# Matmul operands that start at other bytes of a partition than the weights do

## The chip, the cores and the metric

The kernel runs on one core of a Trainium2 chip. The metric is the device time of one execution in microseconds; the kernel before takes 950.53 us, the median of three runs (950.07 to 950.97). All other times are from one execution taken by the hardware profiler, or from the runs.

Engines are named as in the profile: PE is TensorE's matmul, PEld its weight load, DVE is VectorE, ACT is ScalarE, POOL is GpSimd, SP is SyncE, which issues most of the transfers.

## The reference

One layer of a hybrid decoder on 512 positions of width 1024. Cut to what matters:

```python
def reference(x, ...):
    h = rmsnorm(x, norm_mix_g[l])
    proj = h @ w_in[l]                      # 1024 -> 9 x 1024 + gates a, b
    bg, cg, xv, q, k, v, z, a, b, ga, gb = jnp.split(proj, pts, axis=-1)
    y_a = short_conv_branch(bg, cg, xv, conv_a_w[l]) @ w_a_out[l]
    y_b = gdn_branch(q, k, v, z, a, b, ...) @ w_b_out[l]     # chunked gated delta rule
    mix = jax.nn.sigmoid(ga) * y_a + jax.nn.sigmoid(gb) * y_b
    x = x + mix @ w_o[l]
    h = rmsnorm(x, norm_ffn_g[l])
    x = x + conv_ffn(h, w_up[l], ffn_conv_w[l], w_down[l])   # 1024 -> 2 x 2816 -> 1024
    return rmsnorm(x, norm_final_g)
```

All of it is float32.

## The kernel before

Every large product is made of three matmuls in the type fp32r. A float32 operand is split into a high part (the value rounded to fp32r by an ACT copy) and a low part (the rest, by a DVE subtraction), and the product is high times low, low times high, and high times high, summed in one PSUM bank. `mm3` writes this order: first all pairs that mix high and low, then all pairs of high parts. Each call of `mm` (line 109) is one weight load of 128 columns and one matmul that moves 256 or 512 columns past those weights.

The weights of a product come in blocks of 1 MB. A block is loaded into one of two `raw` tiles, and `Block.part` (lines 147 to 151) splits each quarter of 512 columns into a tile `wh` (ACT, line 150) and a tile `wl` (DVE, line 151). There are 12 buffers of each, of 2 KB per partition. `run_jobs` runs the blocks one after the other: the next block is split while PE works on this one, and the one after that is being loaded.

There are two kinds of job. `col_job` multiplies a block as it stands (48 matmuls, of 512 columns mostly). `sum_job` uses sums and differences of quarters, seven products in place of eight (84 matmuls of 256 columns); its moving operands are quarters of the input itself and four sums of quarters, which stand in the tiles `ts` and `us`.

The stages in order of time: the norm of `x`, which leaves the normed input in `hT` (a high and a low tile); q, k, v and z with the delta rule, whose small matmuls are put between the large ones by a count of columns (`tick`, every 2048 columns); gb, cg, xv, bg and ga; the products with `w_a_out` (moving operand `yas`, which lies in pages `kq0`, `KU0` for the high part and `AV0`, `vT`, `Dm` for the low one) and `w_b_out` (moving operand `yb`, the recurrence output); `w_o`; the second norm, which leaves `h2`; up; and down. In `w_o` and down the roles are the other way round: the activations (`mix`, `mixb`, `xs`) are loaded as weights, and `wh` and `wl` move.

Where an operand starts within a partition's memory is fixed when the program is built. In the built program every `wh` and `wl` buffer starts at byte 19424 + 2048 n, and a weight slice of 128 columns at a multiple of 512 bytes from there; `hT` starts at 68576, `h2` at 84960 and 101344. All of these leave 224 when divided by 256. `ts` and `us` are made by `page` and `place` with `up=UP`, 48 elements or 192 bytes past the start of their tile, and leave 160. `yas`, `yb`, `mix` and `xs` start without such an offset and leave 224.

The places that the change touches: `hT`, `h2` and the `yb` parts, allocated as plain tiles of [128, 8, 512]; `split_ya`; `xs`; `raws`, the late weight tiles that reuse the memory of `h2`; and `GT`, a tile of 32 rows which carries the gates' transposed sums to DRAM (`gates_chain`). `junk` is a scratch tile into which `front` throws squares.

Of the kernel before, what the change touches and what calls it, by code (L numbers as in the profile page):

```python
# [9 lines left out]
F32 = mybir.dt.float32  # L10
F32R = mybir.dt.float32r
# [5 lines left out]
P = 128  # L17
S = 512
NT = S // P
D = 1024  # L20
ND = D // P
# [40 lines left out]
def layer_kernel(ctx, tc, x, norm_mix_g, w_in, w_ab, conv_a_w, gdn_conv_w, gdn_A_log, gdn_dt_bias,  # L62
# [14 lines left out]
    def nm(s):  # L77
        cnt[0] += 1
        return f"{s}{cnt[0]}"

    def bank():
        return ps.tile([P, 512], F32, tag="ps", name=nm("ps"))
# [43 lines left out]
    raws = [wp.tile([P, 4, S], F32, bufs=1, name=f"raw{e}") for e in range(2)]  # L126
# [6 lines left out]
    class Block:  # L133
# [21 lines left out]
        def split(self):  # L155
            if self.ready:
                return
            self.ready = True
            for q in range(4):
                self.part(q, self.raw[:, q])  # L160
                yield
# [188 lines left out]
        return SumBlock(lambda: w[i]), use  # L350


    UP = 48

    def place(pool_, tag, name, up=0):
        t = pool_.tile([P, ND * S + 64], F32R, tag=tag, name=name)[:, up:up + ND * S]
        return t.rearrange("p (m a n) -> p m a n", m=4, a=4)

    def split(dst, idx, src):
        act.copy(out=dst[0][:, idx], in_=src)  # L360
# [27 lines left out]

    p1 = ExitStack()
    hp = p1.enter_context(tc.tile_pool(name="hp", bufs=1))  # L390
    hT = [hp.tile([P, ND, S], F32R, tag=f"h{i}", name=f"hT{i}") for i in range(2)]
    yb = hp.tile([P, ND, S], F32, name="yb")


# [4 lines left out]
    def page(tag, name, dtype=F32, up=0):  # L399
        n, more = {"vT": (1024, 64), "Dm": (1024, 64), "kq0": (2048, 64), "KU0": (2048, 64), "AV0": (2048, 64)}.get(tag, (2048, 0))  # L400
        return pg.tile([P, n + more], dtype, tag=tag, name=nm(name))[:, up:up + n]

    def by_columns(t, n=S):
        return t.rearrange("p (k n) -> p k n", n=n)
# [49 lines left out]
    def next_cv():  # L454
        ncv[0] += 1
        return cvs[ncv[0] % 2]
# [201 lines left out]
    gd = p2.enter_context(tc.tile_pool(name="gd", bufs=1))  # L658

    def hn(ap):  # L660
        return ap.rearrange("p (h n) -> p h n", n=NT)

    def prep(pr):
        Dm = by_columns(page("Dm", "Dm"), P)
        nc.sync.dma_start(out=Dm, in_=gtd[8 * pr:8 * pr + 8, :].partition_broadcast(P))
        pool.affine_select(out=Dm, in_=Dm, compare_op=ALU.is_ge, fill=-1e30, base=0,
                           pattern=[[0, 8], [1, P]], channel_multiplier=-1)
        Dms[pr] = Dm
# [10 lines left out]
    def gates_chain(o):  # L679
        abT = next_cv()[0:32]  # L680
        act.copy(out=abT, in_=o[0:32, :])
        yield
        o2 = bank()
        for n in range(NT):
            pe.transpose(out=o2[:, n * 32:(n + 1) * 32], in_=abT[:, n * P:(n + 1) * P], identity=ident[:32, :32])
        ab4 = o2[:, 0:128].rearrange("p (n c) -> p c n", c=32)
        abv = gd.tile([P, 16, NT], F32, name="abv")
        dve.tensor_copy(out=abv, in_=ab4[:, 16:32])
        dve.tensor_tensor(out=abv, in0=abv, in1=ab4[:, 0:16], op=ALU.add)
        T = lambda n: gd.tile([P, 32], F32, tag=n, name=nm(n))  # L690
        u, t, z, q, g = T("u"), T("t"), T("z"), T("q"), T("g")
        dve.tensor_tensor(out=hn(u), in0=abv[:, 0:8, :], in1=dtb.unsqueeze(2).broadcast_to([P, H, NT]), op=ALU.add)
        tc.keep_in_program_order(act.activation(out=hn(beta), in_=abv[:, 8:16, :], func=AF.Exp, scale=-1.0))
        tc.keep_in_program_order(act.activation(out=alg, in_=alg, func=AF.Exp))
        dve.tensor_scalar(t, u, -1.0, None, op0=ALU.mult)
        dve.tensor_tensor(out=t, in0=t, in1=u, op=ALU.min)
        tc.keep_in_program_order(act.activation(out=t, in_=t, func=AF.Exp))
        yield
        pool.tensor_scalar(beta, beta, 1.0, None, op0=ALU.add)
        pool.tensor_scalar(z, t, 2.0, None, op0=ALU.add)  # L700
        yield
        dve.reciprocal(out=beta, in_=beta)
        dve.reciprocal(out=z, in_=z)
        dve.tensor_scalar(u, u, 0.0, None, op0=ALU.max)
        yield
        pool.tensor_tensor(out=t, in0=t, in1=z, op=ALU.mult)
        pool.tensor_tensor(out=z, in0=t, in1=t, op=ALU.mult)
        pool.tensor_scalar(q, z, 1.0 / 15.0, 1.0 / 13.0, op0=ALU.mult, op1=ALU.add)
        for c in (11, 9, 7, 5, 3, 1):
            pool.tensor_tensor(out=q, in0=q, in1=z, op=ALU.mult)  # L710
            pool.tensor_scalar(q, q, 1.0 / c, None, op0=ALU.add)
        pool.tensor_tensor(out=q, in0=q, in1=t, op=ALU.mult)
        pool.tensor_scalar(q, q, 2.0, None, op0=ALU.mult)
        pool.tensor_tensor(out=g, in0=q, in1=u, op=ALU.add)
        pool.tensor_tensor(out=hn(g), in0=hn(g), in1=alg.unsqueeze(2).broadcast_to([P, H, NT]), op=ALU.mult)
        pool.tensor_scalar(g, g, -1.0, None, op0=ALU.mult)
        for _ in range(Y_G):
            yield
        o3 = bank()
        pe.matmul(o3[:, 0:32], lhsT=triu, rhs=g, start=True, stop=True)  # L720
        pe.matmul(o3[:, 32:64], lhsT=ones, rhs=g, start=True, stop=True)
        G, Gl = T("G"), T("Gl")
        dve.tensor_copy(out=G, in_=o3[:, 0:32])
        dve.tensor_copy(out=Gl, in_=o3[:, 32:64])
        dve.tensor_scalar(negG, G, -1.0, None, op0=ALU.mult)
        dve.tensor_tensor(out=kdv, in0=Gl, in1=G, op=ALU.subtract)
        act.activation(out=kdv, in_=kdv, func=AF.Exp)
        act.activation(out=eGl, in_=Gl, func=AF.Exp)
        act.activation(out=eG, in_=G, func=AF.Exp)
        dve.tensor_scalar(neG, eG, -1.0, None, op0=ALU.mult)  # L730
        yield
        o4 = bank()
        pe.transpose(out=o4[0:32, 0:P], in_=G, identity=ident)
        GT = gd.tile([32, P], F32, name="GT")
        dve.tensor_copy(out=GT, in_=o4[0:32, 0:P])
        nc.sync.dma_start(out=gtd, in_=GT)
        prep(0)
# [13 lines left out]
    def tl(n, b=1, shape=(P, 8, P)):  # L751
        return gd.tile(list(shape), F32, tag=n, bufs=b, name=nm(n))
# [371 lines left out]
    def sum_pages():  # L1124
        reach(2, 99)
        his, lows = ([by_columns(t, HS) for n in names for t in halves_of(page(n, "ts", F32R, UP))]
                     for names in (("vT", "Dm", "AV0"), ("kq0", "KU0")))
# [21 lines left out]
    st = {}  # L1149
# [116 lines left out]
        return c  # L1266

    def split_ya():
        st["yas"] = [Rows([by_columns(page(n, "yas", F32R)) for n in names])
                     for names in (("kq0", "KU0"), ("AV0", "vT", "Dm"))]  # L1270
        for k in range(ND):
            split(st["yas"], k, st["ya"][:, k, :])
            yield

    def split_yb():
        st["yb"] = [hp.tile([P, ND, S], F32R, tag=f"h{i}", name=f"yb{i}") for i in range(2)]
        for k in range(ND):
            split(st["yb"], k, yb[:, k, :])
            yield
# [132 lines left out]
    def open_o():  # L1412
        drain(evacs)
        p1.close()
        fp = ctx.enter_context(tc.tile_pool(name="fp", bufs=1))
        st["x1"] = fp.tile([P, NT, D], F32, name="x1")
        st["fp"] = fp
        st["h2"] = [fp.tile([P, ND, S], F32R, tag=f"h2{i}", name=f"h2{i}") for i in range(2)]
        s7 = st["s7"] = p7.enter_context(tc.tile_pool(name="s7", bufs=2))
        gff = st["gff"] = s7.tile([P, D], F32, name="gff", bufs=1)  # L1420
        nc.sync.dma_start(out=gff, in_=norm_ffn_g[0].partition_broadcast(P))
        for t in range(NT):
            nc.sync.dma_start(out=st["x1"][:, t, :], in_=x2[t * P:(t + 1) * P, :])
# [72 lines left out]
    def raw():  # L1496
        return raw_block()
# [8 lines left out]
    def open_up():  # L1506
# [4 lines left out]
        room["pool"], room["o"] = cvp, 2  # L1511
        us.extend(place(up, f"t{i}", f"us{i}", UP) for i in range(2))
        st["aT"] = [up.tile([P, NA, S], F32, name="aTa")]
# [70 lines left out]

    def xs():
        if "xs" not in st:
            st["xs"] = [place(st["up"], f"t{e}", f"xs{e}") for e in range(2)]
        return st["xs"]

    def ffn_pairs(g, n):  # L1590
# [136 lines left out]
    def down_place(i):  # L1727
        def p():
            if i < 2:
                return raw()  # L1730
            if "raws" not in st:
                st["raws"] = [st["fp"].tile([P, 2, 4, S], F32, tag=f"h2{e}", name=f"raws{e}") for e in range(2)]
            e = (i - 2) % 4
            return st["raws"][e // 2][:, e % 2]
        return p
# [61 lines left out]
```

## Time and profile before

| | before |
|---|---|
| median of 3 runs | 950.53 us |
| profiled execution, its own time | 949.49 us |
| its span, first to last instruction | 947.8 us |
| mean granted TensorE clock | 0.996 |
| DVE busy | 778.8 us (82%) |
| ACT busy | 546.9 us (58%) |
| POOL busy | 166.4 us (18%) |
| weight loads busy | 826.8 us (87%) |
| DMA moved | 138.23 MB, mean 146 GB/s |

Matmuls are pipelined, and the profile's duration of one (0.28 us or 0.39 us) reaches into the next; the time that one costs in a dense run is the distance from its start to the next one's start. In the timeline equal instructions in a row are merged: a row has the start of the first, the time to the end of the last, and the count.

### The profile page before, as it was taken

The page shows a single profiled execution, that of the slowest core. Times are in us where ns is not written, and L with a number is a line of the kernel's source. Part 1 is how long each engine was busy: PE and PEld are TensorE (multiplying, and loading weights), DVE is VectorE, ACT ScalarE, POOL GpSimd, SP SyncE. Part 2 cuts the span into 40 slices and gives each one's busy share as a digit, 9 for nine tenths or more (in the row PEclk, how much of TensorE's full clock was granted, in tenths as well). Part 3 has the DMA queues.
Part 4 walks back from the last instruction along what each step waited for, and adds up shares of the span by engine and source line. Part 5 has one row for each costly group of instructions (what it writes and reads, how often), then busy time and mean ns, then how long its engine had stood idle before and what let it go on. Part 6 is the DMA issues. An engine that isn't in the chain of part 4 may idle for free. (4 is left out here: it accounts for less than half of the span.)

```text
span 947.8 us, 17650 instructions
## 1 busy us (share of the span) xinstructions
PE 934.4 (99%) x6512; PEld 826.8 (87%) x6512; DVE 778.8 (82%) x1448; ACT 546.9 (58%) x1202; POOL 166.4 (18%) x280
## 2 busy tenths in 40 slices
PE   8999999999999999999999999999999999999996
PEld 6888887887889999999988888988899998888885
DVE  5978686898978998899753579999899899968875
ACT  6796756666465654555741246466565556556563
POOL 3330401304110022222322000321313110000000
PEclk9999999999999999999999999999999999999999
DMA  6443412213021477776987345575776865087322
GB/s 231 157 139 100 122 54 90 76 50 102 9 91 46 127 191 164 185 197 174 290 219 171 97 153 205 164 191 178 179 174 193 177 135 178 1 294 240 109 91 89
DMA packets 78679, 138.23 MB, mean 146 GB/s; under 512 B 24667, under 2 KB 25600, under 8 KB 76032
## 3 DMA queue, kind: packets, MB, share of 16 engines
q1 hardware_dynamic: 65904, 107.47, 34.8%
q0 software_dynamic: 12544, 29.37, 16.1%
q8 instruction: 51, 0.84, 0.3%
q14 instruction: 36, 0.29, 0.1%
q10 hardware_dynamic: 144, 0.26, 0.1%
HBM read 133.64 MB, written 32.78 MB: 176 GB/s over the span
## 5 line engine op out<-in xcount | busy, mean ns | idle before, releaser
L150 ACT CAST wh<-raw 128x512 fp32r<-128x512 f32 x377 | 223.2, 620 | 184.0 <-PE ps L109 115.3
L109 PE MATMUL ps<-hT,wh 128*128 128x512 f32 (+1 forms) x1048 | 283.1, 350 | 1.1 <-ACT hT L570 0.8
L151 DVE TENSOR_TENSOR wl<-raw,wh 128x512 fp32r<-128x512 f32 x377 | 250.6, 685 | 36.3 <-ACT wh L150 33.1
L109 PEld LDWEIGHTS ps<-hT,wh 128*128 128x128 f32 x1048 | 183.4, 190 | 21.6 <-ACT hT L570 1.1
L109 PE MATMUL ps<-hT,wl 128*128 128x512 f32 (+1 forms) x524 | 172.5, 343 | 0.0
L109 PE MATMUL ps<-h,wh 128*128 128x256 f32 (+1 forms) x688 | 168.4, 333 | 0.0
L109 PEld LDWEIGHTS ps<-h,wh 128*128 128x128 f32 x688 | 118.5, 189 | 12.5
L109 PEld LDWEIGHTS ps<-hT,wl 128*128 128x128 f32 x524 | 99.6, 190 | 9.7
L109 PE MATMUL ps<-h,wl 128*128 128x256 f32 (+1 forms) x344 | 108.0, 332 | 0.0
L109 PE MATMUL ps<-ts,wh 128*128 128x256 f32 x544 | 100.8, 280 | 0.0
L109 PE MATMUL ps<-wh,xs 128*128 128x512 f32 (+1 forms) x320 | 96.6, 384 | 0.0
L109 PEld LDWEIGHTS ps<-ts,wh 128*128 128x128 f32 x544 | 85.1, 188 | 0.4 <-ACT u L338 0.2
L173 DVE TENSOR_TENSOR raw<-raw 128x512 f32<-128x512 f32 x108 | 74.2, 687 | 2.0
L109 PEld LDWEIGHTS ps<-h,wl 128*128 128x128 f32 x344 | 65.2, 189 | 6.2
L109 PEld LDWEIGHTS ps<-wh,xs 128*128 128x128 f32 x320 | 59.7, 188 | 11.8
L109 PE MATMUL ps<-ts,wl 128*128 128x256 f32 x272 | 65.7, 277 | 0.0
L109 PE MATMUL ps<-wl,xs 128*128 128x512 f32 (+1 forms) x160 | 61.5, 384 | 0.0
L237 POOL COPY gate<-raw 1x1 f32<-1x1 f32 x38 | 15.6, 411 | 254.2 <-DMA raw<-in_w_up_dram 100.1
L109 PE MATMUL ps<-us,wh 128*128 128x256 f32 x320 | 58.2, 278 | 0.7 <-ACT v L341 0.7
L367 DVE SCALAR_TENSOR_TENSOR ct<-ps,wA,ct 128x511 f32<-128x511 f32 (+2 forms) x72 | 53.1, 740 | 4.0 <-ACT ct L364 3.8
L150 ACT CAST wh<-raws 128x512 fp32r<-128x512 f32 x66 | 39.6, 620 | 25.6 <-DVE wl L151 8.1
L151 DVE TENSOR_TENSOR wl<-raws,wh 128x512 fp32r<-128x512 f32 x66 | 43.2, 686 | 11.6 <-ACT wh L150 11.5
(340 smaller groups left out, 1641.0 us busy)
## 6 DMA issues: line engine op xcount, KB each, us to landing
raw<-in_w_up_dram SPq DMA_DIRECT2D x88, 256.0 KB, 4.4
raw<-in_w_in_dram SPq DMA_DIRECT2D x20, 1024.0 KB, 5.1
raw<-in_w_in_dram SPq DMA_DIRECT2D x64, 256.0 KB, 4.5
dv<-in_w_down_dram POOLq DMA_DIRECT2D x50, 256.0 KB, 6.5
raws<-in_w_down_dram SPq DMA_DIRECT2D x32, 256.0 KB, 3.7
raws<-dv SPq DMA_DIRECT2D x24, 256.0 KB, 5.3
ov<-in_w_o_dram POOLq DMA_DIRECT2D x20, 256.0 KB, 6.2
raw<-in_w_a_out_dram SPq DMA_DIRECT2D x16, 256.0 KB, 5.0
```

The costliest lines, as they stand in the source:

```text
L109: pe.matmul(o, lhsT=a, rhs=b, start=start, stop=stop, skip_group_check=free)
L150: act.copy(out=wh, in_=src)
L151: dve.tensor_tensor(out=wl, in0=src, in1=wh.bitcast(F32), op=ALU.subtract)
L173: dve.tensor_tensor(out=r[q], in0=a, in1=b, op=op)
L237: tc.keep_in_program_order(pool.tensor_copy(out=gate[:, 0:1], in_=el[:, 0:1]))
L367: dve.scalar_tensor_tensor(out=dst[:, sh:], in0=src[:, :S - sh], scalar=wcol(j), in1=dst[:, sh:], op0=ALU.mult, op1=ALU.add)
```

## The change

The tiles of the moving operands get 64 elements more (256 bytes per partition), and the operand starts some elements into its tile: `hT` and `h2` 32 elements (128 bytes), `yb` 40 (160 bytes), the low part of `yas` 32, `xs` 32. The high part of `yas`, `mix` and `mixb` stay, and so do `ts` and `us` with their 48. To make room, `GT` loses its own tile and uses `junk`. `raws` is allocated in the same larger form, without an offset.

```diff
-    UP = 48
+    UP, H_AT, YA_AT, YB_AT, X_AT = 48, 32, 32, 40, 32
...
+    def rows_at(pool_, tag, name, up=0, dtype=F32R):
+        t = pool_.tile([P, ND * S + 64], dtype, tag=tag, name=name)[:, up:up + ND * S]
+        return t.rearrange("p (k n) -> p k n", n=S)
...
-    hT = [hp.tile([P, ND, S], F32R, tag=f"h{i}", name=f"hT{i}") for i in range(2)]
+    hT = [rows_at(hp, f"h{i}", f"hT{i}", H_AT) for i in range(2)]
...
-        GT = gd.tile([32, P], F32, name="GT")
+        GT = tl("junk", 1, (P, P))[0:32]
...
-        st["yas"] = [Rows([by_columns(page(n, "yas", F32R)) for n in names])
-                     for names in (("kq0", "KU0"), ("AV0", "vT", "Dm"))]
+        st["yas"] = [Rows([by_columns(page(n, "yas", F32R, at)) for n in names])
+                     for at, names in ((0, ("kq0", "KU0")), (YA_AT, ("AV0", "vT", "Dm")))]
...
-        st["yb"] = [hp.tile([P, ND, S], F32R, tag=f"h{i}", name=f"yb{i}") for i in range(2)]
+        st["yb"] = [rows_at(hp, f"h{i}", f"yb{i}", YB_AT) for i in range(2)]
...
-        st["h2"] = [fp.tile([P, ND, S], F32R, tag=f"h2{i}", name=f"h2{i}") for i in range(2)]
+        st["h2"] = [rows_at(fp, f"h2{i}", f"h2{i}", H_AT) for i in range(2)]
...
-            st["xs"] = [place(st["up"], f"t{e}", f"xs{e}") for e in range(2)]
+            st["xs"] = [place(st["up"], f"t{e}", f"xs{e}", X_AT) for e in range(2)]
...
-                st["raws"] = [st["fp"].tile([P, 2, 4, S], F32, tag=f"h2{e}", name=f"raws{e}") for e in range(2)]
+                st["raws"] = [rows_at(st["fp"], f"h2{e}", f"raws{e}", dtype=F32).rearrange("p (a q) n -> p a q n", a=2)
+                              for e in range(2)]
```

In the built program the operands' remainders by 256 become 96 for `hT`, `h2`, `xs` and the low part of `yas`, and 128 for `yb`; the weights keep 224. The matmuls, and all instructions of the other engines, stand in the same order as before. One wait is new. On ACT, at the first square of `front` (about 50 us into the program; the line numbers differ by four), there stands before:

```order
L727 ACTIVATE kdv<-kdv 128x32 [waits DVE_49]
L728 ACTIVATE eGl<-Gl_652 128x32
L1074 CAST kqs_528<-kq_527 128x512 [waits Activation_49]
L777 ACTIVATE junk_692,ssk_689<-ps_695 128x128 [waits PE_49]
L364 ACTIVATE ct_107<-ps_622,wA 128x512 [waits PE_49]
```

and now:

```order
L731 ACTIVATE kdv<-kdv 128x32 [waits DVE_49]
L732 ACTIVATE eGl<-Gl_652 128x32
L1078 CAST kqs_528<-kq_527 128x512 [waits Activation_49]
L781 ACTIVATE junk_692,ssk_689<-ps_695 128x128 [waits DMAHW4_49,PE_49]
L368 ACTIVATE ct_107<-ps_622,wA 128x512 [waits PE_49]
```

Nothing moved; the first write of `junk` now waits for the transfer of `GT` to DRAM as well, which reads the same memory.

## The prediction

> **What bounds the kernel now.** I read the page's busy times, its 40 slices and its chain first, then the groups of PE instructions, and then single starts in the timeline, since a busy PE says nothing about how fast it streams. From the page, busy times, PE's slices (tenths) and the shares of the chain that ended last:
>
> ```profile
> PE 934.4 (99%) x6512; PEld 826.8 (87%) x6512; DVE 778.8 (82%) x1448; ACT 546.9 (58%) x1202; POOL 166.4 (18%) x280
> ...
> PE   8999999999999999999999999999999999999996
> ...
> PE 16%; DVE 1%; ACT 1%; DMA 1%; issue 0%; POOL 0%; POOLq 0%; ACTq 0%; SPq 0%
> ```
>
> PE is idle for 947.8 - 934.4 = 13.4 us of the span, and only its first and last slices are under nine tenths. The chain that ended last is PE wherever it could be followed. So the time is the number of matmuls times the distance between two starts, and a change of that distance counts nearly in full.
>
> The counts that matter here are in the groups by line, name, count, busy time and mean ns (both column counts together in the first six rows; the names are output, moving operand and weights, in no fixed order):
>
> ```profile
> L109 PE MATMUL ps<-hT,wh 128*128 128x512 f32 (+1 forms) x1048 | 283.1, 350 | 1.1 <-ACT hT L570 0.8
> L109 PE MATMUL ps<-hT,wl 128*128 128x512 f32 (+1 forms) x524 | 172.5, 343 | 0.0
> L109 PE MATMUL ps<-h,wh 128*128 128x256 f32 (+1 forms) x688 | 168.4, 333 | 0.0
> L109 PE MATMUL ps<-h,wl 128*128 128x256 f32 (+1 forms) x344 | 108.0, 332 | 0.0
> L109 PE MATMUL ps<-wh,xs 128*128 128x512 f32 (+1 forms) x320 | 96.6, 384 | 0.0
> L109 PE MATMUL ps<-wl,xs 128*128 128x512 f32 (+1 forms) x160 | 61.5, 384 | 0.0
> ...
> L109 PE MATMUL ps<-yb,wh 128*128 128x512 f32 x128 | 39.6, 389 | 0.0
> L109 PE MATMUL ps<-yas,wh 128*128 128x512 f32 x128 | 39.6, 389 | 0.0
> ...
> L109 PE MATMUL ps<-yb,wl 128*128 128x512 f32 x64 | 24.9, 389 | 0.0
> ```
>
> The distances come from the timeline of the up stage, where `h2` (shown as `h`) stands at the same remainder by 256 bytes as the weights, and `us` 192 bytes further:
>
> ```profile
> 734.88 0.28 PE L109 MATMUL ps<-h,wl 128*128 128x256 f32 x1
> 734.88 0.19 PEld L109 LDWEIGHTS ps<-h,wh 128*128 128x128 f32 x1
> ...
> 736.64 0.73 PE L109 MATMUL ps<-us,wh 128*128 128x256 f32 x5
> ...
> 737.21 0.28 PE L109 MATMUL ps<-us,wl 128*128 128x256 f32 x1
> ...
> 742.10 2.20 PE L109 MATMUL ps<-h,wh 128*128 128x512 f32 x9
> ...
> 744.14 0.39 PE L109 MATMUL ps<-h,wl 128*128 128x512 f32 x1
> ...
> 750.30 0.76 PE L109 MATMUL ps<-h,wh 128*128 128x256 f32 x5
> ...
> 750.90 0.28 PE L109 MATMUL ps<-h,wl 128*128 128x256 f32 x1
> ```
>
> Three numbers follow. With 512 columns of `h`, (744.14 - 742.10) / 9 = 226.7 ns a matmul. With 256 columns of `h`, (750.90 - 750.30) / 5 = 120.0 ns. With 256 columns of `us`, (737.21 - 736.64) / 5 = 114.0 ns. The first two differ by 106.7 ns for 256 columns, so beside its columns a matmul of `h` costs 226.7 - 2 x 106.7 = 13.3 ns whether it is long or short, and one of `us` costs 114.0 - 106.7 = 7.3 ns. The first pair of rows says what could make that difference: the weights of the next matmul are loaded from the very moment at which this one starts. Two reads of the same memory run side by side, and where both start at the same remainder by 256 bytes, 6.0 ns more are lost than at 192 bytes further.
>
> **The change part by part.** Moved operands: hT 1048 + 524, h 688 + 344, xs 320 + 160, yb 128 + 64, and 64 of yas, since only the low part moves, which `mm3` pairs once with each high weight slice (half of the row of 128). That is 1572 + 1032 + 480 + 192 + 64 = 3340 matmuls. In down the loaded and the moving side change places, but the distance between both becomes 128 bytes there too.
>
> What a matmul costs at 128 or at 160 bytes no row shows; rows show 0 and 192 only. The bounds are 13.3 ns of gain (nothing but the columns is left) and none, or a loss of the same 6.0 ns if 128 is worse than 0. I take the row it is nearest to, `us`: 128 and 160 lie 64 and 32 bytes from 192, and 128 and 96 from 0. The gain is then 6.0 ns, for long and short matmuls alike, since the load of 128 columns lies beside the first part of either. 3340 x 6.0 ns = 20.0 us.
>
> From the Trainium skill, "TensorE: Matmul & The Clock Gate", Back-to-back issue gap: a matmul in a row costs N / 2.4 plus some 2.5 ns. The trace agrees on the columns (256 / 2.4 = 106.7) and not on the rest (13.3 and 7.3 ns); if its 2.5 ns were reached at 128 bytes, an estimate from that page would be 10.8 ns a matmul, 36 us.
>
> What doesn't reach the end: first, places where PE is held by a chain through other engines. Between 757.5 and 776.8 us the chain of waits leaves PE (start, us, what; in order of time):
>
> ```profile
> 757.51 0.49 DVE wl L151
> ...
> 765.84 5.49 DMA raw<-in_w_up_dram
> ...
> 776.35 0.38 ACT v L341
> ...
> 776.78 153.66 PE ps L109 x729
> ```
>
> DVE frees a raw tile, the next block is loaded for 5.49 us, ACT and DVE work it up, and PE waits. In those 19.3 us PE's share of the gain (20.0 / 947.8 x 19.3 = 0.4 us) is lost. Second, stretches where DVE is nearly full, from the table by stretches:
>
> ```profile
> 380.00:440.00 60.00, 60.00 (x519) 60.00 (x518) 57.15 (x91) 32.26 (x69) 14.31 (x24) 1.00 0.70 183
> ...
> 600.00:640.00 40.00, 40.00 (x277) 37.38 (x276) 39.35 (x58) 22.01 (x38) 12.60 (x18) 1.00 0.70 180
> 640.00:700.00 60.00, 60.00 (x396) 55.00 (x395) 55.26 (x87) 33.41 (x64) 13.75 (x24) 1.00 0.67 174
> ```
>
> Columns after the stretch: its length, then busy times of PE, PEld, DVE, ACT and POOL. From 380 to 440 us DVE has 2.85 us to spare, more than the 1.3 us that a 60 us stretch would gain. From 600 to 640 us it has 0.65 us against a gain of 0.8 us; weights split ahead (12 buffers) cover that, and if the cover is gone, 0.2 us stay lost. From 640 us it has 4.7 us. Third, the delta rule in the first 320 us. Its groups of PE with hT, and from 100 to 200 us the longest wait of DVE's recurrence for PE:
>
> ```profile
> L109 PE MATMUL ps<-hT,wh 128*128 128x512 f32 x512 | 169.3, 403 | 0.0
> L109 PE MATMUL ps<-hT,wl 128*128 128x512 f32 x256 | 100.4, 392 | 0.0
> L109 PE MATMUL ps<-hT,wh 128*128 128x256 f32 x152 | 32.7, 295 | 1.1 <-ACT hT L570 0.8 <-DVE hT L574 0.3
> ...
> L109 PE MATMUL ps<-hT,wl 128*128 128x256 f32 x76 | 20.0, 287 | 0.0
> ...
> DVE vn L997 <- PE ps L995: 3.6, 4, 1.7
> ```
>
> These are 996 of the 3340, 6.0 us of the gain (the last row shows the recurrence waiting for PE 4 times, 3.6 us in all, so there PE is the late one). The delta rule's small matmuls stand at fixed counts of columns between large ones; when the large ones go faster, a step's DVE and ACT work has less cover. A loss of a quarter, 1.5 us, is my choice between nothing and all 6.0.
>
> The `GT` edit: the copy into `junk` takes the place of the copy into `GT`, and ACT's first square waits for the transfer. From the timeline, and from the answer on the tile GT:
>
> ```profile
> 46.29 0.32 SPq L736 DMA_DIRECT2D gtd<-GT  x1
> ...
> 50.11 0.27 ACT L777 ACTIVATE junk<-ps 128x128 f32<-128x128 f32 x1
> ...
> DMA to landing us min/median/max: 1.4/1.4/1.4
> ```
>
> It lands 1.4 us after 46.29, so at 47.7 us, 2.4 us before ACT gets to the square: nothing. If it landed late, ACT's conv work and the splits queue behind that square, and PE behind them. Larger tiles add no instruction, and `raws` keeps its form: nothing. Weights are asked for 2% sooner; the two raw tiles cover it except at 765.84, counted above.
>
> Sum: 20.0 - 0.4 - 0.2 - 1.5 = 17.9 us. The profiled execution's own 949.49 us would be 931.6; it stands 1.04 us under the median of the runs, so for the median 950.53 - 17.9 = **932.6 us**.
>
> **The rivals.**
>
> *Further apart is better still.* If the loss falls evenly with the distance up to half of 256 bytes, the two rows (13.3 at 0, 7.3 at 64 the other way round) give 1.3 ns at 128 and 4.3 at 160: a gain of 12.0 ns for 3148 matmuls and 9.0 for 192, 39.5 us. The losses double, 0.8 and 3.0 us, and DVE lacks 1.0 us from 600 to 640 us, 4.8 us together: 915.8. For it: the two rows fit a straight line, with so few points any line would. Against it: nothing shows that 7.3 isn't the floor.
>
> *The places repeat every 128 bytes.* The rows show 0 and 192; 192 is 64 past a multiple of 128, and 128 would be 0 again. Only yb (160) gains, 192 x 6.0 = 1.2 us: 949.4. Against it speaks nothing in the rows of before.
>
> *The place is not the cause.* The 6.0 ns between `h` and `us` would come from something else that the tiles differ in (h is laid out in rows of 512 columns, us in blocks of 256). Nothing changes then: 950.5. For it: place and layout differ together in these rows. Against it: both move 256 adjacent columns. From the Trainium skill, the same page, Step-by-step: weights and moving operand have independent read ports, and loading "doesn't steal SBUF read bandwidth from the running matmul". By that rule this rival holds; the trace, with 120.0 against 114.0 ns, shows a loss that the rule doesn't know, though not yet whose.
>
> *Some groups gain and others not*, since in down the loaded side lies behind and not ahead, and at 512 columns no shifted row exists: without xs (480) and with half of the rest, 1430 x 6.0 = 8.6, less 1: 943.
>
> *Worse at 128.* The side that reads behind may meet the other one more often at 128 than at 0, by the mirror of the 6.0 ns: 3340 x 6.0 = 20 us on PE's path, 970.5. It decides from 227 and 120 ns upwards. Nothing speaks for it but that the rows show only two places.
>
> *The change doesn't move what it says*: the built program has remainders 96 and 128 beside the weights' 224, so this is out.
>
> **How the numbers follow.** Forecast 62%, better still 18%, some groups 8%, repeating at 128 5%, another cause 3%, worse 4%. A measurement of this kernel can tell about 0.2%, 1.9 us, from no change. Faster by more: 62 + 18 + 8 = 88%; within: 5 + 3 = 8%; slower: 4%. The range goes from 916, the better case, to 945, past the partial one; left out are the two without effect, the worse one and what of the better one is better yet, under two in ten. The likeliest case's own range is 927 (7.3 ns gained and little lost) to 937.
>
> **What would show it.** In the timeline of the up stage, 512 columns of `h` at about 220.7 ns in place of 226.7, 256 columns at 114, and `us` still at 114; in down 220.7 too; `yb` and hT the same. mix and mixb keep 226.7. PE's waits from 757 to 777 us grow by about 0.4 us. At 214 to 216 ns the better case holds; at 226.7 one of the two without effect, and the tiles that moved, against yb, tell which. If the distances are at 220.7 and the time is above 937, the losses were mis-sized, and PE's idle time in the first 320 us and in the up stage tells where. A wait of ACT near 50 us would show that `GT` costs something.

## The result, and the profile after

The changed kernel takes **959.49 us**, the median of three runs (958.74 to 960.96), against 950.53 (950.07 to 950.97): the ratio is 1.0097, with a 95% interval of 1.0074 to 1.0120. It is 9.0 us slower, where 17.9 us of gain were forecast. The profiled execution of after has a span of 959.3 us, 11.5 us over that of before; that is 2.5 us more than between the medians, since the profiled execution of before lies 1.0 us under its median and that of after 1.5 us over.

From the page of after, the busy times and the shares of the chain:

```profile
PE 946.2 (99%) x6512; PEld 826.8 (86%) x6512; DVE 779.8 (81%) x1448; ACT 547.7 (57%) x1202; POOL 170.2 (18%) x280
...
PE 17%; DVE 1%; ACT 1%; DMA 1%; issue 0%; POOL 0%; POOLq 0%; ACTq 0%; SPq 0%
```

PE idles for 959.3 - 946.2 = 13.1 us, where it was 13.4. So none of the 11.5 us is a new wait: PE is busy 946.2 - 934.4 = 11.8 us longer with the same 6512 matmuls, while the weight loads' busy time is the same to a tenth. The longer time is in the distances between matmuls. Three groups of PE (line, names, count, busy time, mean ns of one) say in which:

```profile
L109 PE MATMUL ps<-wh,xs 128*128 128x512 f32 (+1 forms) x320 | 98.5, 389 | 0.0
L109 PE MATMUL ps<-yb,wh 128*128 128x512 f32 x128 | 40.5, 396 | 0.0
L109 PE MATMUL ps<-wh,mix 128*128 128x512 f32 x88 | 28.1, 391 | 0.0
```

`yb` and `xs` went from 389 to 396 and from 384 to 389 ns; `mix`, which wasn't moved, has the same row in before. The mean of a row is a duration and not a distance, so the size is read from single starts. The timeline of after, the up stage first (start, length of the merged row, names, count), then two rows of down:

```profile
736.18 0.76 PE L109 MATMUL ps<-h,wh 128*128 128x256 f32 x5
736.77 0.28 PE L109 MATMUL ps<-h,wl 128*128 128x256 f32 x1
...
739.02 0.75 PE L109 MATMUL ps<-us,wh 128*128 128x256 f32 x5
739.61 0.28 PE L109 MATMUL ps<-us,wl 128*128 128x256 f32 x1
...
743.23 0.73 PE L109 MATMUL ps<-us,wh 128*128 128x256 f32 x5
743.80 0.28 PE L109 MATMUL ps<-us,wl 128*128 128x256 f32 x1
...
748.78 2.26 PE L109 MATMUL ps<-h,wh 128*128 128x512 f32 x9
750.88 0.39 PE L109 MATMUL ps<-h,wl 128*128 128x512 f32 x1
...
905.09 0.63 PE L109 MATMUL ps<-wh,xs 128*128 128x512 f32 x2
...
908.59 0.63 PE L109 MATMUL ps<-wh,xs 128*128 128x512 f32 x2
```

512 columns of `h` take (750.88 - 748.78) / 9 = 233.3 ns; they took 226.7. The two rows of `xs` are 15 matmuls apart: 3.50 / 15 = 233.3 too. 256 columns of `h` take 0.59 / 5 = 118 ns, 2 less than before. And `us`, which the change doesn't touch, has two values now: 118 ns in one run, 114 in another.

Means of all distances of a group, from the single starts in both traces (ns; in brackets the number of distances, those whose next matmul is of line 109 too). Of the short ones, the few of 200 ns and more are left out; the longest, of 0.8 and 1.0 us, hold a wait of PE:

| group | before | after | sum, us |
|---|---|---|---|
| 512 columns: `h` (480) | 226.9 | 233.2 | +3.0 |
| `hT` (782) | 235.6 | 239.6 | +3.1 |
| `xs` (456) | 226.7 | 233.3 | +3.0 |
| `yb` (192) | 226.7 | 234.3 | +1.5 |
| `yas` (192, a third of them moved) | 226.7 | 229.1 | +0.5 |
| 256 columns: `h` (543), `hT` (678) | 119.3, 119.3 | 118.8, 118.7 | -0.3, -0.4 |
| `ts` (795), `us` (479), not moved | 114.5, 114.3 | 115.7, 115.4 | +0.9, +0.5 |

These add up to 11.8 us, as much as PE's busy time grew. Long matmuls lost, short ones gained a little, and short ones that nobody moved lost.

The rest of what the prediction looked at stands as it said or nearly. The transfer of the gates from the timeline, with ACT's first square; then the chain of waits of the up stage:

```profile
45.45 0.33 SPq L740 DMA_DIRECT2D gtd<-junk  x1
...
49.19 0.27 ACT L781 ACTIVATE junk<-ps 128x128 f32<-128x128 f32 x1
```

```profile
764.47 0.47 DVE wl L151
...
772.80 5.92 DMA raw<-in_w_up_dram
...
783.73 0.38 ACT v L341
...
784.16 160.54 PE ps L109 x741
```

The square comes 3.7 us after the issue, with no wait noted before it. The stretch of the chain takes 784.16 - 764.47 = 19.7 us, 19.3 before; its transfer takes 5.92 us, 5.49 before.

### The profile page after: what moved, and what is told of

The parts are those of the page before. It is cut to its first block, busy times and chain, and to the rows that moved or that the text cites. A ratio compares the mean times of both kernels' runs of the same rounds, so it can differ in the third digit from the quotient of the medians.

```text
span 959.3 us, 17651 instructions
## 1 busy us (share of the span) xinstructions
PE 946.2 (99%) x6512; PEld 826.8 (86%) x6512; DVE 779.8 (81%) x1448; ACT 547.7 (57%) x1202; POOL 170.2 (18%) x280
## 5 line engine op out<-in xcount | busy, mean ns | idle before, releaser
L109 PE MATMUL ps<-h,wh 128*128 128x256 f32 (+1 forms) x688 | 170.4, 335 | 0.0
L237 POOL COPY gate<-raw 1x1 f32<-1x1 f32 x38 | 19.9, 524 | 251.7 <-DMA raw<-in_w_up_dram 98.5
L151 DVE TENSOR_TENSOR wl<-raws,wh 128x512 fp32r<-128x512 f32 x66 | 43.5, 686 | 12.9 <-ACT wh L150 11.8
```

The lines of the kernel that those rows point to most:

```text
L109: pe.matmul(o, lhsT=a, rhs=b, start=start, stop=stop, skip_group_check=free)
L151: dve.tensor_tensor(out=wl, in0=src, in1=wh.bitcast(F32), op=ALU.subtract)
L237: tc.keep_in_program_order(pool.tensor_copy(out=gate[:, 0:1], in_=el[:, 0:1]))
```

## The experiments

Each kernel but the four measurements was timed beside the kernel before on the same chip; where an interval is given, the ratio is to that.

**1. Places, by themselves.** The layer is left out. PE alone runs 24 matmuls in a row, each with its own weight load, in the same type; `at` moves one operand in steps of 16 bytes, once with 512 columns and once with 256. In `both` runs weights and operand move together ("same") or 128 bytes apart ("far").

```python
def run(n, m_at, w_at, count, name):
    o = ps.tile([P, 512], F32, tag="ps", name=name)
    for k in range(count):
        w = W[:, w_at + P * (k % 8):w_at + P * (k % 8) + P]
        m = M[:, m_at + S * (k % 4):m_at + S * (k % 4) + n]
        pe.matmul(o[:, 0:n], lhsT=w, rhs=m, start=k == 0, stop=k == count - 1)
...
for n, kind in ((S, "long"), (S // 2, "short")):
    for at in range(0, 64, 4):
        run(n, at, 0, 24, kind + "abcdefghijklmnop"[at // 4])
```

> The kernel's computation is left out: runs of 24 matmuls in fp32r, 128 rows by 512 (long) or 256 (short) columns, nothing beside them, with the moving operand 0, 16, ... 240 bytes from the weights by 256 bytes, then at the same and at 128 bytes with both moved by 32, 64, 96, 128 bytes. Theory R, the cost is set by the distance between moving operand and weights, and long matmuls have another best place than short ones: long 226.5 ns at 0 and 233 at 128, short 120 at 0, 113.5 at 192 and 120 at 128, and the runs with both moved repeat 226.5 and 233. Theory A, the moving operand's own place in memory sets it: with both moved the numbers change, although the distance is the same. Theory E, other engines' reads and writes make the difference: here all places cost the same.

The timeline of this kernel; the letters a, b, i, m are 0, 16, 128 and 192 bytes, and a distance is the difference of two following starts by 24:

```profile
11.75 5.60 PE L64 MATMUL longa<-M,W 128*128 128x512 f32 x24
17.19 5.72 PE L64 MATMUL longb<-M,W 128*128 128x512 f32 x24
...
56.15 5.75 PE L64 MATMUL longi<-M,W 128*128 128x512 f32 x24
61.74 5.76 PE L64 MATMUL longj<-M,W 128*128 128x512 f32 x24
...
100.80 3.03 PE L64 MATMUL shorta<-M,W 128*128 128x256 f32 x24
103.67 3.02 PE L64 MATMUL shortb<-M,W 128*128 128x256 f32 x24
...
134.84 2.89 PE L64 MATMUL shortm<-M,W 128*128 128x256 f32 x24
137.57 3.02 PE L64 MATMUL shortn<-M,W 128*128 128x256 f32 x24
...
179.29 5.64 PE L64 MATMUL bothdsame<-M,W 128*128 128x512 f32 x24
184.77 5.76 PE L64 MATMUL bothdfar<-M,W 128*128 128x512 f32 x24
```

Long matmuls: (17.19 - 11.75) / 24 = 226.7 ns at 0 and (61.74 - 56.15) / 24 = 232.9 at 128. Of the sixteen places only 0 and 240 have 227; 64 has 229, and the other thirteen lie between 230.8 and 234.6. Short ones: 119.6 ns at 0, 118.3 at 128, 113.8 at 192; of the others 112 is as low (113.3), and the rest lie between 117 and 120. With the weights moved as well, the distance is 227.5 to 228.3 when both move together (the pair shown: 228.3) and 233 where they are 128 apart: for these long matmuls it is the difference of the two places that counts, not the place of either. What after shows in its up stage, 233.3 and 118, is what PE does here with nothing beside it. The reasons by which other engines, queues or the larger tiles would have slowed it aren't needed.

**2. All of the change, but every distance 0.** Larger tiles, `GT` in `junk`, `raws` by `rows_at`:

```diff
-    UP, H_AT, YA_AT, YB_AT, X_AT = 48, 32, 32, 40, 32
+    UP, H_AT, YA_AT, YB_AT, X_AT = 48, 0, 0, 0, 0
```

> The changed kernel with all new offsets at 0: larger tiles, GT in junk, and the operands where they were. Theories R and A: within 0.3% of before, 950.5. Theory G, the larger tiles or GT's wait cost the 9 us: 957 or more, and 226.7 ns at 512 columns.

949.74 us against 949.42: ratio 1.0001 (0.9990 to 1.0012). So, to within 1 us, all of the loss comes from the distances, none from the tiles or from `GT`.

**3. and 4. All at 192, all at 64.** The same line with 48, 48, 48, 48, 48, and with 48, 16, 16, 16, 16.

> All new offsets at 48 elements (192 bytes), where ts and us are. Theory R: the 1284 short matmuls fall from 120 to 113.5 ns, 8 us; the 2056 long ones are open: 226.7 would give 943, the 233 of the changed kernel 956, a fall of 6 ns 931. If 192 is good for all, the choice of 128 was the fault; if long ones are over 226.7 here too, moving long operands is.

> All new offsets at 16 elements (64 bytes). If distance counts alike in both directions, as 192 bytes: short 113.5 ns. If the direction counts, short at 118 to 121 and long at 226 to 240 ns; total between 945 and 962.

At 192 it takes 956.77 us, ratio 1.0062 (1.0044 to 1.0081); at 64, 953.05 in a single run beside a median of 949.42. The timeline of the kernel with 192, in the up stage:

```profile
748.20 2.27 PE L109 MATMUL ps<-h,wh 128*128 128x512 f32 x9
750.30 0.39 PE L109 MATMUL ps<-h,wl 128*128 128x512 f32 x1
...
756.61 0.75 PE L109 MATMUL ps<-h,wh 128*128 128x256 f32 x5
757.20 0.28 PE L109 MATMUL ps<-h,wl 128*128 128x256 f32 x1
```

Long `h` is at 233.3 ns here as well, and short `h` at 118: at the very distance at which `us` had 114.0 in before, a short matmul isn't at 114. `us` itself, unmoved, has a mean of 117.8 too. But the short matmuls of `hT`, moved to the same distance in the same kernel, have a mean of 114.2 (119.3 before, both without distances of 200 ns and more), and `ts` keeps 113.9. So the gain at 192 came for `hT` and not for `h`: even the row that the prediction took as nearest is no property of the place alone.

In down the loaded side is the one that is moved, and there the long values of these two kernels change places: `xs` has 228.9 ns at 192 and 233.3 at 64, `h` 233.2 and 229.1. That is what a difference with its sign gives, for weights 192 bytes up leave the operand at 64, and weights 64 up at 192.

**5. A finer scale.** The measurement of experiment 1 with steps of 4 bytes, around 0 and around 112.

```diff
-        for at in range(0, 64, 4):
-            run(n, at, 0, 24, kind + "abcdefghijklmnop"[at // 4])
+        for i in range(22):
+            run(n, 64 + i - 18, 0, 24, kind + "abcdefghijklmnopqrstuv"[i])
```

> The kernel's computation is left out: runs of 24 matmuls with nothing beside them, in steps of one element (4 bytes) from 184 to 268 bytes past the weights by 256 bytes, long (512 columns) and short (256), and short ones from 100 to 124 bytes too. Theory L, there are narrow places at which a row of matmuls locks into its best rhythm: long 226.7 ns in a band around 0 that holds 240 and ends before 224 and 16, short 113.3 ns in a band of a few elements around 192 and around 112; the rest 228 to 236 and 116 to 121. Theory W, wide and smooth: neighbouring places differ by under 1 ns, and the bands are tens of bytes.

The timeline, long matmuls at 240 and 244 bytes (o, p), and at 252, 0 (which is 256), 4 and 8 (r to u):

```profile
90.44 5.81 PE L64 MATMUL longo<-M,W 128*128 128x512 f32 x24
96.08 5.92 PE L64 MATMUL longp<-M,W 128*128 128x512 f32 x24
...
107.50 5.69 PE L64 MATMUL longr<-M,W 128*128 128x512 f32 x24
113.03 5.61 PE L64 MATMUL longs<-M,W 128*128 128x512 f32 x24
118.48 5.86 PE L64 MATMUL longt<-M,W 128*128 128x512 f32 x24
124.18 5.75 PE L64 MATMUL longu<-M,W 128*128 128x512 f32 x24
```

235.0 ns at 240; then 230.4 at 252, 227.1 at 0 and 237.5 at 4. Of these 22 places one of 4 bytes is the floor for long matmuls, with 3 and 10 ns more one step beside it. Outside of it the values go up and down every 16 bytes: 229.6 to 232.1 ns at 188, 204, 220, 236, 252 and 268, and 236.3 to 240.0 at 196, 212, 228 and 244. And 240, which had 227 in experiment 1, has 235 here; short ones at 192 have 117.9 here, and had 113.8 there. The same place gives two values. The two kernels differ there in what ran before, and they ran on different chips; experiment 8 has both values of the short ones in one execution.

**6. 240 bytes for `hT` and `h2`,** the second good place of experiment 1, all else at 0 (48, 60, 0, 0, 0). This was a try for a faster kernel.

> hT and h2 240 bytes past the weights, all other new offsets 0. From the single places (long 226.7 ns at 240 as at 0, short 116.9 in place of 119.7): 1260 short matmuls by 2.8 ns, 3.5 us less than before, 946; if matmuls between the large ones break the rhythm, between 946 and 952.

A miss: 957.86 us, ratio 1.0094 (1.0078 to 1.0110). Long `h` has a mean of 236.5 ns, near the 235.0 of experiment 5 and not the 227 of experiment 1.

**7. The change without `hT` and `h2`** (48, 0, 32, 40, 32).

> The change without its part on hT and h2: yb at 160, low yas and xs at 128 bytes. By the distances of the single places (long 226.7 at 0, 232.5 to 233.5 at 128, 234.1 at 160): xs 456, yb 192 and yas 64, by 6.8 ns, 4.8 us more than before, 955; the part left out, hT and h2, then holds the other 4 us. If the parts don't add up, something other than the matmuls' distances carries it.

954.31 us against 948.61, ratio 1.0053 (1.0035 to 1.0071), 5.0 us by the ratio. `xs`, `yb` and `yas` move only long matmuls and hold over half of the loss, as the table of distances says (3.0 + 1.5 + 0.5). `hT` and `h2`, long and short together and with what they do to `ts` and `us`, are left with the other 4 us. Here, with `h` back at 0, `ts` and `us` are within 0.2 ns of their means of before (again without distances of 200 ns and more).

**8. What ran before.** PE alone again: runs of 24 behind runs of another kind; copies of the kernel's sum jobs, in which parts at 192 stand between parts at 0, 128 or 192 (`job`); and weights of 32 to 128 columns (`cols`). In the code a pair is a number of columns and a place in elements of 4 bytes; S is 512 and H 256.

```python
befores = {"afterlongzero": (S, 0), "afterlongfar": (S, 32), "aftershortzero": (H, 0), "aftershortfar": (H, 32)}
for kind, target in (("short", (H, 48)), ("long", (S, 60)), ("longfar", (S, 32)), ("longzero", (S, 0))):
    for name, (n, at) in befores.items():
        run(n, at, 0, 24, "x" + name)
        run(*target, 0, 24, kind + name)
```

> The kernel's computation is left out: runs of matmuls with nothing beside them. First each of four targets (short at 192, long at 240, 128 and 0 bytes) right after a run of 24 at four other places. Theory H, the rhythm depends on how a run is entered: short at 192 gives 113.3 ns after some and 117 to 118 after others, long at 240 gives 226.7 after some and 235 after others; long at 0 always settles at 226.7, long at 128 at 233. Theory N, only the place counts: each target has one value whatever went before. Then copies of a sum job, 24, 24, 12, 24 short matmuls with the second and fourth part at 192 and the others at 0, 128 or 192: if H, the parts at 192 cost 113 to 114 ns beside 0 and 116 to 118 beside 128. Last, long matmuls with 32, 64, 96 and 128 columns of weights, at 0 and 128: if each 16 bytes of a weight load take one cycle of 0.417 ns from the moving read, at 0 the matmul costs 213.3 plus 3.3, 6.7, 10.0 and 13.3 ns; if the cost beside the columns is a fixed 13.3 ns, all are 226.7.

Its timeline; in a `job`, a and c stand at the place that is named (`far` is 128) and b and d at 192:

```profile
16.87 2.99 PE L64 MATMUL shortafterlongzero<-M,W 128*128 128x256 f32 x24
19.70 5.75 PE L64 MATMUL xafterlongfar<-M,W 128*128 128x512 f32 x24
25.29 2.88 PE L64 MATMUL shortafterlongfar<-M,W 128*128 128x256 f32 x24
28.01 3.02 PE L64 MATMUL xaftershortzero<-M,W 128*128 128x256 f32 x24
...
191.23 2.99 PE L64 MATMUL jobfarb<-M,W 128*128 128x256 f32 x24
194.06 1.59 PE L64 MATMUL jobfarc<-M,W 128*128 128x256 f32 x12
195.48 2.88 PE L64 MATMUL jobfard<-M,W 128*128 128x256 f32 x24
198.20 11.06 PE L64 MATMUL plainup<-M,W 128*128 128x512 f32 x48
...
218.99 5.71 PE L64 MATMUL colszeroa<-M,W 128*32 128x512 f32 x24
224.53 5.69 PE L64 MATMUL colszerob<-M,W 128*64 128x512 f32 x24
```

The same 24 short matmuls at 192 take 117.9 ns each behind long ones at 0 and 113.3 behind long ones at 128. Between parts at 0 both parts at 192 have 114.2 ns. Between parts at 128 the first one has (194.06 - 191.23) / 24 = 117.9 and the second one (198.20 - 195.48) / 24 = 113.3: that is the 118 and the 114 that the unmoved `us` shows in after, where of its 20 runs of 24 matmuls 8 are at 118 and 11 at 113 to 114 (in before 19 are at 114). Long matmuls at 0 and at 128 keep their value behind all four: 226.7 to 228.8 at 0, 232.5 to 233.3 at 128. Long ones at 240 have 233.3 to 236.3 behind all four, so the 227 of experiment 1 didn't come back, and why it was there once stays open. The last two rows speak against a cost that grows with the bytes of the load: a load of 32 columns has 5.54 / 24 = 230.8 ns beside it, no less than one of 128 columns.

**9. The sum jobs' weights 64 bytes up, their operands at 0.** The difference is 192 again, but for short matmuls alone, with all long ones left at 0. To fit, the weights have 11 buffers; `UP` is 0, and `GT` stands in `junk`. `at` is 16 elements for the sum jobs' blocks and 0 for the others.

```diff
-WQ = 12
+WQ = 11
...
-            wh = wp.tile([P, S], F32R, tag="wh", bufs=WQ, name=nm("wh"))
-            wl = wp.tile([P, S], F32R, tag="wl", bufs=WQ, name=nm("wl"))
+            wh = wp.tile([P, S + 64], F32R, tag="wh", bufs=WQ, name=nm("wh"))[:, self.at:self.at + S]
+            wl = wp.tile([P, S + 64], F32R, tag="wl", bufs=WQ, name=nm("wl"))[:, self.at:self.at + S]
```

> Moving operands stay where they were before, and the weights of the sum jobs move: 64 bytes up in their buffers, with ts and us at no offset, so that all short matmuls of sum jobs stand at 192 and all long ones at 0 (11 weight buffers in place of 12 make room, GT in junk). Theory N: about 1040 short matmuls of h and hT fall from 121 to 113.5 ns, 7 us less, 942. Theory H: those at 192 lock only when entered well; between 943 and 952. If 11 buffers are too few, PE waits and the time is over 952 with the distances as said.

952.09 us, ratio 1.0035 (1.0022 to 1.0048): no gain. Without distances of 200 ns and more, `h` has a mean of 118.4 and `hT` of 116.8 ns (119.3 both before), `ts` 116.6 and `us` 117.8 (114.5 and 114.3 before): the last two lose more than the first two gain.

**10. and 11. The same, entered by one product at 0, and the 11 buffers alone.** Experiment 8 suggested that a stretch at 0 ahead would bring the 113 ns; so product "11" of a sum job keeps its weights unshifted. Beside it, the kernel before with only `WQ = 11`.

```diff
+            at = 0 if name == "11" else self.at
```

> As the run with the sum jobs' weights moved, but the first of a sum job's seven products keeps its weights unmoved: 12 short matmuls at 0 between the long ones at 0 and the 72 short ones at 192. Theory H: entered from short at 0, the rest locks at 113.3 to 114 ns; the two later products of h and hT in each sum job (about 640 matmuls) fall from 121 to 114, ts and us come back from 118 to 115: 4 to 7 us under the run before it, 945 to 948. Theory N, place alone: at 192 still 117.7, and 952 to 953.

> The kernel before with 11 weight buffers of each kind in place of 12 and nothing else. If the buffers cost nothing: within 0.2% of before. If they cost what the run with moved weights lost beside the distances: 2 to 4 us more, and a wait of PE for DVE of 2 to 3 us in the first 60 us.

The first is a miss: 953.97 us, ratio 1.0051 (1.0038 to 1.0065), short ones still at 117.5 to 118.8 ns. The 11 buffers alone give 951.42 us, ratio 1.0033 (1.0017 to 1.0049), about as much as all that experiment 9 lost. In the waits of PE (line, what it waited for, us, times, longest) that kernel has one that before hasn't, and the kernel of experiment 9 has it too, with 2.9 us:

```profile
PE ps L109 <- DVE KU L778: 3.6, 1, 3.6
```

**12. Entry, and which side is moved.** PE alone: 24 long matmuls at 0, then k short ones at 0, then 24 short ones at a difference of 192, k from 0 to 16; the difference is made by the moving operand (`moving`) or by the weights (`weights`).

```python
for k in range(17):
    name = "abcdefghijklmnopq"[k]
    run(S, 0, 0, 24, "x" + name)
    if k:
        run(H, 0, 0, k, "y" + name)
    run(H, 48, 0, 24, "moving" + name)
for k in (4, 8, 12, 16):
    ...
    run(H, 0, 16, 24, "weights" + name)
```

> The kernel's computation is left out: 24 long matmuls at 0, then k short ones at 0 (k from 0 to 16), then 24 short ones at 192, the moving operand shifted (and for k of 4, 8, 12 and 16 once more with the weights shifted by 64 bytes). Theory H says that entry decides: the last 24 cost 117.7 ns for k = 0 and 113.3 ns for some k, 117.7 for others, so that a job that puts 12 at 0 ahead, as the last version did, can miss. If 113.3 came whenever at least one short matmul at 0 went ahead, that version should have locked, and something else in the kernel breaks the rhythm; if the shifted weights give 117.7 where the shifted moving operand gives 113.3, it matters which side was shifted, and distance alone is not enough.

Its timeline, `moving` with k = 0 and k = 12, then `weights` with k = 12:

```profile
17.17 2.99 PE L64 MATMUL movinga<-M,W 128*128 128x256 f32 x24
20.00 5.60 PE L64 MATMUL xb<-M,W 128*128 128x512 f32 x24
...
124.96 2.90 PE L64 MATMUL movingm<-M,W 128*128 128x256 f32 x24
127.70 5.62 PE L64 MATMUL xn<-M,W 128*128 128x512 f32 x24
...
192.30 2.99 PE L64 MATMUL weightsm<-M,W 128*128 128x256 f32 x24
195.13 5.63 PE L64 MATMUL xwq<-M,W 128*128 128x512 f32 x24
```

117.9 ns with k = 0 (and 1), 114.2 with every k from 2 to 16, and 117.9 with the weights moved, at all four k tried. So two short matmuls at 0 ahead are enough, if the operand is the side that moves; if the weights are, none of the four tried brings the lower value. This fits the misses of experiments 9 and 10, where the weights were moved; that it is all of their cause isn't shown.

## Why the prediction was wrong

**Where it was right.** PE sets the end, and a change of the distance counts in full: 11.8 us of distances, 11.8 of PE's busy time, 11.5 of the span. `GT`, the larger tiles and `raws` cost nothing (experiment 2). `mix` kept its group mean. The chain of 19.3 us grew by the 0.4 us that were forecast, but by luck: its transfer took 0.4 us longer, and PE wasn't faster. Nor was the reading right that PE waits in those 19.3 us: by the traces it was busy for 18.55 of 19.27 us there in before, and for 18.94 of 19.72 in after. The losses of 0.2 and 1.5 us were never put to the test, since nothing became faster.

**The step that failed** is this one: "I take the row it is nearest to, `us`: 128 and 160 lie 64 and 32 bytes from 192, and 128 and 96 from 0. The gain is then 6.0 ns, for long and short matmuls alike". Three things in it didn't hold.

- *Nearness.* Nothing changes smoothly between 0 and 192. For long matmuls 0 is the floor, and 4 bytes away on one side 10 ns are lost, on the other 3 (experiment 5); 128 and 160 lie on the plain of 231 to 234 ns.
- *Long and short alike.* The 6.0 ns came from short matmuls alone; no row of before had a long one at another place. Long ones at 192 lose as they do at 128 (233.3 ns, experiment 3). That 13.3 ns stand beside the columns "whether it is long or short" was no finding: the 106.7 ns for 256 columns had been worked out from the long and the short row at 0, which makes the rest of both equal. At 128 the same sum gives 233.3 - 2 x 106.7 = 19.9 for a long one and 118 - 106.7 = 11.3 for a short one. The least that any run leaves beside the columns by that sum is 13.3 ns for long ones and 113.3 - 106.7 = 6.6 for short ones, so the 2.5 ns on which the 36 us of the prediction rest were never seen.
- *The place as a property of one matmul.* `us` had 114.0 behind short matmuls at 0. Moving `h` took that away from `us` and `ts` in part of their runs (experiments 7 and 8), 1.4 us that the prediction had counted at nothing ("`us` still at 114").

Of the rivals, *worse at 128* had the sign and nearly the size (4.0 to 7.6 ns for long matmuls, by the table, where all of a group moved), and got 4%. It priced all 3340 matmuls; only the long ones pay, some 2000, and the moved short ones give 0.7 us back. At its 6.0 ns the long ones alone would have been some 12 us; they paid 3.0 + 3.1 + 3.0 + 1.5 + 0.5 = 11.1. The remark against it, that the rows show only two places, was equally a remark against the forecast: with one measured gain, at another length, the bounds of 13.3 ns of gain and 6 of loss were the finding, and the chances should have lain much nearer to even.

*Further apart is better still*, *the places repeat every 128 bytes* and *some groups gain* are out by the same measurement: alone on PE, long matmuls have 232.9 ns at 128 and 233.8 at 160, and no moved group of long ones gained.

*The place is not the cause* is out by experiment 1. From the Trainium skill, "TensorE: Matmul & The Clock Gate", Step-by-step: weights and moving operand have read ports of their own, and a load takes no read bandwidth from the running matmul. By that rule the place of the one against the other should not matter. The runs disagree: 226.7 against 232.9 ns by place alone, with PE alone at work. That it is the two reads that meet is not shown by them.

**What stays open.** What makes these values is not settled. A clash of the two reads that costs by the bytes of the load is out, since a load of a quarter of the columns costs no less (experiment 8); and no fixed price of a place will do, since one sequence of places gives two values by how it was entered. That a dense run falls into one of several rhythms and stays in it describes this, but no run shows what keeps the rhythm, nor why the side that is moved matters, nor why `hT` had the lower value at 192 in experiment 3 and `h` had not. No version here was faster than the kernel before. Not tried: `hT` and `h2` held twice, at 0 for long and at 192 for short matmuls.

## What to carry to other kernels

A matmul's distance to the next can depend on where its operand starts relative to the weights, and a value measured at one length and place says nothing of another length or a place in between: measure each pair that the change will use, in the sequence of the kernel, before counting it times three thousand. A run of PE alone with the places in question showed the sign in 191 us of chip time, and a second one behind other runs showed where a good value holds. When a rival is only "unsupported", ask whether the forecast rests on more rows than it does.

## What was not expected of the hardware

- For 512 columns in fp32r with a load for each matmul, one place of 4 bytes among the 22 tried from 184 to 268 has 227 ns, its neighbours 230.4 and 237.5, and the values off it go up and down every 16 bytes (experiment 5).
- 24 equal matmuls at equal places take 113.3 or 117.9 ns each by what ran ahead of them (experiment 8).
- For 256 columns a difference of 192 bytes is 114.2 ns when the moving operand makes it, and 117.9 when the weights make it, each behind 4 to 16 matmuls at 0 (experiment 12).
- A weight load of 32 columns in place of 128 makes the distance no shorter: 230.8 against 226.7 ns (experiment 8; the latter is the run of 128 columns at the same place).
